# One core of Trainium2, two transformer blocks with a mixture of experts: a narrow expert's transposes moved behind the wide one's second products, seven load buffers filled by halves, norm rows asked for sooner

## Chip, core, metric

The kernel runs on one core of one Trainium2 chip. The metric is the device time of one execution in microseconds; the number that stands for a kernel is the median of its runs. Engines are named as the profile names them: PE (TensorE), DVE (VectorE), ACT (ScalarE), POOL (GpSimd), SP (SyncE). Each takes its instructions in the order in which they stand in its own queue.

## What is computed

256 positions of width 1024 pass through two layers of a first block (a mixer, then a feed-forward part, each closed by a layer norm) and one layer of a second block. Layer 0 has a dense feed-forward part, layer 1 a mixture of 8 experts. All data are fp32. The parts that the change touches, cut down:

```python
def swiglu(x, w1, w3, w2):
    return (silu(x @ w1) * (x @ w3)) @ w2

def moe_swiglu(x, router_w, w1, w3, w2):           # 8 experts, each position uses 2
    top_v, top_i = top_k(x @ router_w, 2)
    combine = sum(one_hot(top_i, 8) * softmax(top_v)[..., None], axis=1)
    return sum(combine[:, e:e + 1] * swiglu(x, w1[e], w3[e], w2[e]) for e in range(8))

for layer in range(2):
    x = layer_norm(ALPHA * x + hybrid_mixer(x, ...), ln1_g[layer], ln1_b[layer])
    f = moe_swiglu(x, ...) if layer else swiglu(x, ...)   # 1024 -> 3584 -> 1024 per expert
    x = layer_norm(ALPHA * x + f, ln2_g[layer], ln2_b[layer])
# second block
x = x + mixer_2(rms_norm(x, norm1_g))
x = x + conv_ffn(rms_norm(x, norm2_g))
return rms_norm(x, final_g)
```

## The kernel before

The program runs straight through: layer 0's mixer (0 to 225 us of the profiled span), its dense feed-forward part (225 to 411), layer 1's mixer (425 to 650), the experts (650 to 1632), the norms behind them (to 1658), the second block's front (to 1782) and its feed-forward part (to the end).

Weights are read from HBM in loads of 2 MB (128 partitions by 4096 numbers) into buffers called `raw`, all issued by SP (`load`, L151). A weight that meets 128 positions or more is split by `split` (L158) into a high part `wH` (cast by ACT, L170) and a low part `wL` (a subtraction, L172, on DVE or on POOL where `hold` says so), and `mm3` (L175) makes three products of them: L176, L177, L178.

The experts go in four groups of two. Of each pair one is wide: it is given 128 slots for positions, uses split weights, and its names are `main`, `hH`, `hL`. The other is narrow: it has 64 slots, takes the raw fp32 weights straight into PE (`side`, L1243, matmuls of L1247), and its names are `nar`, `gx`, `hN`. (One group has an expert with 192 slots instead.) An expert's hidden width of 3584 is cut into seven pieces of 512. A step of `experts` (L1281) does for one piece: two loads and the first products with w1 and w3 (L1302 to L1310); silu on ACT (L1316 wide, L1321 narrow) and the product of the two on DVE (L1317, L1322); then `down`, the second products, of the step before, with a third load `rd` (L1325); then the transposes of this step's result (L1331 wide, L1339 narrow, both recorded at L182), which ACT copies out (`hN`, L1342) or splits. Wide and narrow steps take turns, so a cycle is one of each: six loads. When a narrow step ends its first products, the second products that follow it are those of the wide step ahead of it: 24 matmuls with the name `acc`. A scheduler settles each engine's order from the program and its dependences; `issue_after(x)` binds an instruction behind x if both are on the same engine.

While the experts run there are six buffers, three in the pool `wp` and three in `mp` (L1360).

A layer norm (L258 to L271) runs per half of the positions, `t`: statistics on DVE, the inverse root by `rsqrt` (L184: one DVE operation and POOL's power, L188), then on DVE one operation over 1024 columns (L268) and a pair of 128x512 (L270). `rms` (L286) is alike, with its pair at L300. `layer_norm` and `rms` give back `p`, the rsqrt; `finish` (L312) transposes the result and puts into `hold` that the next splits of weights on POOL come after `p`. This is so at four places: behind the mixer of layer 0, behind its feed-forward part, behind the experts, and in the second block's front. The norm behind the experts takes its rows of gains and offsets by `row` (L273), DMAs that ACT issues: `g` ahead of the branch for overfull experts (L1389), `b` and `g2` behind it (L1396).

## Time and profile before

| | us |
|---|---|
| median of 3 runs | 2001.44 (1994.93 to 2006.64) |
| the profiled execution | 2001.22 |
| its span, first to last instruction | 1999.4 |
| busy: PE, DVE, ACT, POOL | 1819.5, 1197.6, 842.3, 203.4 |
| experts' loads | 168 of 2 MB |

The profile is one execution on the chip. Busy times are sums over an engine's instructions; an engine's idle time counts only where it holds up what sets the end. The rows further down come from six views: the page (shares by engine, DMA issues), waits (how long an engine stood still, and for what), the timeline (instruction by instruction: start, length, engine, line, operation, and in brackets the idle time before it and what ended it), windows (busy time, granted clock of PE and DMA by stretch), groups by line, and the DMA queue's own waits. [...]

### The profile page before, as it was taken

To read this page: it belongs to the slowest core of one execution; us is meant where nothing else is said; L and a number is where in the kernel's file an instruction comes from. 1 tells how busy PE (TensorE), PEld (TensorE's weight loads), DVE (VectorE), ACT (ScalarE), POOL (GpSimd) and SP (SyncE) were. 2 spreads that over 40 slices of the span, in tenths; PEclk is the share of its full clock that TensorE was granted. 3 is DMA by queue.
4 is the path that set the end of the run, shared out by engine and by line. 5 is a ranking of instruction groups with operands and counts; after the bars stand their busy time and mean duration, and the time that the engine had idled before them with its cause. 6 is when DMAs were issued, how large, how long until landed. Compare 5 with 4: busy or idle time off the path is not lost. (4 is left out here: it accounts for less than half of the span.)

```text
span 1999.4 us, 28155 instructions
## 1 busy us (share of the span) xinstructions
PE 1819.5 (91%) x11670; PEld 1408.2 (70%) x11670; DVE 1197.6 (60%) x1717; ACT 842.3 (42%) x1176; POOL 203.4 (10%) x128
## 2 busy tenths in 40 slices
PE   7778899986878999998989999999999868989998
PEld 6666899975656766666666666666666637779997
DVE  6796654578785755355454544344553647667776
ACT  3234344433243545334343443343443525545554
POOL 4251200043323000000000000000000004010000
PEclk9788999998788999999999999999999988799999
DMA  6320536352204799999999777787999944134551
GB/s 241 118 94 23 190 137 243 127 215 85 95 13 169 282 430 418 388 393 355 363 393 384 300 297 305 307 342 315 365 414 390 399 156 164 43 135 171 185 195 64
DMA packets 37574, 484.76 MB, mean 242 GB/s; under 512 B 4544, under 2 KB 5184, under 8 KB 8000
## 3 DMA queue, kind: packets, MB, share of 16 engines
q1 hardware_dynamic: 34992, 475.74, 60.8%
q10 hardware_dynamic: 2448, 7.17, 1.1%
q8 instruction: 93, 1.52, 0.3%
q14 instruction: 41, 0.34, 0.0%
HBM read 481.84 MB, written 1.05 MB: 242 GB/s over the span
## 5 line engine op out<-in xcount | busy, mean ns | idle before, releaser
L172 DVE TENSOR_TENSOR wL<-raw,wH 128x1024 fp32r<-128x1024 f32 (+1 forms) x510 | 616.3, 1229 | 261.9 <-ACT wH L170 250.7
L170 ACT CAST wH<-raw 128x1024 fp32r<-128x1024 f32 x560 | 577.5, 1051 | 401.7 <-PE mm L177 154.0
L1247 PE MATMUL mm<-raw,gx 128*64 128x256 f32 x2240 | 252.3, 381 | 0.0
L1247 PEld LDWEIGHTS mm<-raw,gx 128*64 128x64 f32 x2240 | 156.6, 137 | 85.6 <-issue 10.8
L176 PE MATMUL acc<-wH,hH 128*128 128x512 f32 x408 | 163.8, 416 | 19.8 <-ACT wH L170 19.0
L176 PE MATMUL mm<-wH,g 128*128 128x512 f32 x448 | 177.1, 395 | 0.0
L177 PE MATMUL acc<-wL,hH 128*128 128x512 f32 x408 | 169.7, 416 | 7.2 <-DVE wL L172 7.1
L177 PE MATMUL mm<-wL,g 128*128 128x512 f32 x448 | 175.1, 391 | 0.0
L178 PE MATMUL mm<-wH,g 128*128 128x512 f32 x448 | 174.8, 390 | 0.0
L178 PE MATMUL acc<-wH,hL 128*128 128x512 f32 x408 | 166.8, 410 | 0.0
L172 POOL TENSOR_TENSOR wL<-raw,wH 128x1024 fp32r<-128x1024 f32 x50 | 126.1, 2532 | 135.2 <-ACT wH L170 122.3
L188 POOL TENSOR_TENSOR sm_brs<-sm_brs,half_neg 128x1 f32<-128x1 f32 x8 | 12.1, 1518 | 1207.2 <-DVE sm_brs L186 1207.2
L1247 PE MATMUL acc<-raw,hN 128*64 128x512 f32 x560 | 127.5, 597 | 0.0
L1321 ACT ACTIVATE ff<-mm 128x256 f32<-128x256 f32 x35 | 13.5, 385 | 247.8 <-PE mm L1247 247.8
L176 PEld LDWEIGHTS acc<-wH,hH 128*128 128x128 f32 x408 | 79.1, 197 | 44.4 <-ACT wH L170 22.5
L177 PE MATMUL mm<-b2yL,wH 128*128 128x256 f32 x384 | 109.7, 286 | 0.0
L176 PE MATMUL mm<-b2yH,wH 128*128 128x256 f32 x384 | 109.6, 286 | 0.0
L178 PE MATMUL mm<-b2yH,wL 128*128 128x256 f32 x384 | 109.4, 285 | 0.0
L1322 DVE TENSOR_TENSOR ff<-ff,mm 128x256 f32<-128x256 f32 x35 | 14.7, 421 | 157.2 <-ACT ff L1321 157.2
L177 PEld LDWEIGHTS acc<-wL,hH 128*128 128x128 f32 x408 | 80.2, 197 | 32.3 <-DVE wL L172 14.7
L176 PE MATMUL mm<-y0H,wH 128*128 128x256 f32 x352 | 100.1, 285 | 0.0
L178 PE MATMUL mm<-y0H,wL 128*128 128x256 f32 x352 | 99.8, 284 | 0.0
(518 smaller groups left out, 3263.2 us busy)
## 6 DMA issues: line engine op xcount, KB each, us to landing
raw<-in_moe_dram SPq DMA_DIRECT2D x168, 2048.0 KB, 9.7
raw<-in_ffn_dram SPq DMA_DIRECT2D x33, 2048.0 KB, 7.7
raw<-in_w_in_dram SPq DMA_DIRECT2D x13, 2048.0 KB, 9.2
raw<-in_w_o_dram SPq DMA_DIRECT2D x4, 2048.0 KB, 7.5
row<-in_ln_dram ACTq DMA_DIRECT2D x8, 512.0 KB, 3.6
raw<-in_w_out_dram SPq DMA_DIRECT2D x2, 2048.0 KB, 8.4
raw<-in_w_in_dram SPq DMA_DIRECT2D x3, 1024.0 KB, 5.1
raw<-in_ffn_dram SPq DMA_DIRECT2D x3, 1024.0 KB, 5.2
```

The lines of the kernel that those rows point to most:

```text
L170: self.A.copy(H, src)
L172: (eng or self.V).tensor_tensor(L, src, H.bitcast(F32), OP.subtract)
L176: self.T.matmul(out, lhsT=lh, rhs=rh, start=start, stop=False)
L177: self.T.matmul(out, lhsT=lh, rhs=rl, start=False, stop=False)
L178: return self.T.matmul(out, lhsT=ll, rhs=rh, start=False, stop=stop)
L188: return self.G.tensor_tensor(out, out, self.half_neg.to_broadcast([P, n]), OP.pow)
L1247: T.matmul(out[i * 64:i * 64 + 64], lhsT=lhsT, rhs=rhs[:, i * n:i * n + n], start=start, stop=stop)
L1321: A.activation(sn[-1], b[:, 0:256], AF.Silu)
L1322: V.tensor_tensor(sn[-1], sn[-1], b[:, 256:512], OP.mult)
```

## The change

1. `RAWS` = 4 load buffers in `wp` instead of 3, in the whole kernel. The experts take seven fixed tiles in turn (four of `wp`, three of `mp`), and such a tile is filled by two DMAs of 1 MB.
2. The narrow expert's transposes are bound behind the last matmul of piece j = 2 of the second products that `down` has just put out.
3. Gain and offset of the norm behind the experts go into one tile `gb` by two DMAs ahead of the branch.
4. `p`, behind which POOL's held splits come, is the last DVE operation of the norm instead of the rsqrt on POOL.
5. The program is built with a smaller scratch space for DMAs issued from engines.

```diff
@@ __init__
-        self.raws = [(self.wp, 3)]
+        self.raws = [(self.wp, RAWS)]
@@ load
-        self.nc.sync.dma_start(raw[:, :n], ap)
+        m = n if isinstance(src, tuple) else n // 2
+        for o in range(0, n, m):
+            self.nc.sync.dma_start(raw[:, o:o + m], ap[:, o:o + m])
         return raw
@@ layer_norm
-        p = self.rsqrt(rs, mv[:, 1:2], 1.0, LN_EPS)
+        self.rsqrt(rs, mv[:, 1:2], 1.0, LN_EPS)
         V.scalar_tensor_tensor(r[:, t], r[:, t], mv[:, 0:1], g, op0=OP.subtract, op1=OP.mult)
         for n in range(2):
-            V.scalar_tensor_tensor(r[:, t, half[n]], r[:, t, half[n]], rs, b[:, half[n]], op0=OP.mult, op1=OP.add)
-        return p
+            last = V.scalar_tensor_tensor(r[:, t, half[n]], r[:, t, half[n]], rs, b[:, half[n]], op0=OP.mult, op1=OP.add)
+        return last
@@ rms
         for n in range(2):
-            self.V.scalar_tensor_tensor(dst[:, t, half[n]], xn[:, t, half[n]], ss[:, 0:1], g[:, half[n]], op0=OP.mult, op1=OP.mult)
-            yield half[n]
+            yield self.V.scalar_tensor_tensor(dst[:, t, half[n]], xn[:, t, half[n]], ss[:, 0:1], g[:, half[n]], op0=OP.mult,
+                                              op1=OP.mult)
@@ experts, down
-                            self.mm3(acc[n], h[0][:, j], h[1][:, j], H[:, 0, ns], L[:, 0, ns], *ends)
+                            last = self.mm3(acc[n], h[0][:, j], h[1][:, j], H[:, 0, ns], L[:, 0, ns], *ends)
+                        if j == 2:
+                            state["down"] = last
@@ experts
             for (p, b), s in zip(nar, sn):
-                b = self.bank()
+
+                b, last = self.bank(), state.pop("down", None)
                 for i in range(2):
-                    self.transpose(b[:, i * P:(i + 1) * P], s[:, i * P:(i + 1) * P])
+                    with self.tc.issue_after(last.ins) if last else nullcontext():
+                        self.transpose(b[:, i * P:(i + 1) * P], s[:, i * P:(i + 1) * P])
@@ moe
-        self.raws, self.chunk = [(self.wp, 3)] * 3 + [(self.mp, MORE)] * MORE, 0
+
+        self.raws = [p.tile([P, 4096], F32, tag="raw", name=f"raw{n}x{i}", bufs=n) for p, n in (
+            (self.wp, RAWS), (self.mp, MORE)) for i in range(n)]
+        self.chunk = 0
...
-        self.raws = [(self.wp, 3)]
-        ahead = self.block2_loads(0, 3)
-        g = self.row(a["ln"][1, 2], "rscr")
+        self.raws = [(self.wp, RAWS)]
+        ahead = self.block2_loads(0, RAWS)
+        gb = self.xp.tile([P, 2, D], F32, tag="xTL", name="gb", bufs=1)
+        for i in range(2):
+            A.dma_start(gb[:, i], a["ln"][1, 2 + i].partition_broadcast(P))
...
-        self.raws = [(self.wp, 3)]
-        b, g2 = self.row(a["ln"][1, 3], "yL"), self.row(a["rows2"][0], "yH")
+        self.raws = [(self.wp, RAWS)]
+        g2 = self.row(a["rows2"][0], "yH")
...
-            self.layer_norm(xn, t, g, b)
+            self.layer_norm(xn, t, gb[:, 0], gb[:, 1])
         for t in range(2):
-            p, *_ = self.rms(xn, t, g2, h)
+            *_, p = self.rms(xn, t, g2, h)
@@ block 2, front
-        left = self.block2_loads(3, 4)
+        left = self.block2_loads(RAWS, 4)
...
-            p = next(rms[t])
+            next(rms[t])
         for r in rms:
-            list(r)
+            *_, p = r
```

PE, a cycle of the second group before: `gx` are the narrow expert's first products, `ff` the transposed result, `wH` and `wL` the wide expert's second products.

```order
L1247 MATMUL mm_7794<-raw_7788,gx_7125 64x256 x16
L1247 MATMUL mm_7794<-raw_7790,gx_7125 64x256 x16
L182 MATMUL mm_7870<-cst_4_126,ff_7827 128x128 x2
L176 MATMUL acc_7437<-wH_7830,hH_7784 128x512
L176 MATMUL acc_7438<-wH_7830,hH_7784 128x512
L177 MATMUL acc_7437<-wL_7831,hH_7784 128x512
```

The same cycle after the change (lines are three or seven higher; of the 24 second products the first and the last stand here):

```order
L1250 MATMUL mm_7606<-raw4x_5604,gx_7132 64x256 x16
L1250 MATMUL mm_7606<-raw4x_5605,gx_7132 64x256 x16
L179 MATMUL acc_7444<-wH_7642,hH_7596 128x512
L179 MATMUL acc_7445<-wH_7642,hH_7596 128x512
L180 MATMUL acc_7444<-wL_7643,hH_7596 128x512
...
L181 MATMUL acc_7444<-wH_7672,hL_7597 128x512
L180 MATMUL acc_7445<-wL_7673,hH_7596 128x512
L181 MATMUL acc_7445<-wH_7672,hL_7597 128x512
L185 MATMUL mm_7682<-cst_4_126,ff_7639 128x128 x2
L179 MATMUL mm_7693<-wH_7695,g_7131 128x512
```

The two transposes stand behind all 24 second products instead of ahead of them.

ACT, a cycle of the first group before: L1316 is the wide silu, L1321 the narrow one, L1342 the copy of the transposed narrow result, `wH` from the first raw the casts of the second products' weights.

```order
L1316 ACTIVATE ff_6585<-mm_6503 128x512
L170 CAST hH_6601<-mm_6596 128x512
L1321 ACTIVATE ff_6644<-mm_6611 128x256
L1342 COPY hN_6690<-mm_6687 128x256
L170 CAST wH_6647<-raw_6609 128x1024
L170 CAST wH_6657<-raw_6609 128x1024
L170 CAST wH_6667<-raw_6609 128x1024
L170 CAST wH_6677<-raw_6609 128x1024
L170 CAST wH_6700<-raw_6692 128x1024
```

After:

```order
L1321 ACTIVATE ff_6787<-mm_6705 128x512
L173 CAST wH_6767<-raw3x_5609 128x1024
L173 CAST wH_6777<-raw3x_5609 128x1024
L173 CAST hH_6803<-mm_6798 128x512
L1326 ACTIVATE ff_6846<-mm_6813 128x256
L173 CAST wH_6849<-raw4x_5606 128x1024
L173 CAST wH_6859<-raw4x_5606 128x1024
L173 CAST wH_6869<-raw4x_5606 128x1024
L173 CAST wH_6879<-raw4x_5606 128x1024
L173 CAST wH_6902<-raw3x_5607 128x1024
L173 CAST wH_6912<-raw3x_5607 128x1024
L1349 COPY hN_6892<-mm_6889 128x256
```

The copy moved from ahead of the casts to behind six of them; the casts stay behind the narrow silu.

POOL behind the experts, before: `sm_brs` and `sm_rms` are the rsqrts of the layer norm and of the rms norm, `wL` the two held splits.

```order
L188 TENSOR_TENSOR sm_brs_20595<-sm_brs_20595,half_neg 128x1
L188 TENSOR_TENSOR sm_brs_20606<-sm_brs_20606,half_neg 128x1
L188 TENSOR_TENSOR sm_rms_20612<-sm_rms_20612,half_neg 128x1
L188 TENSOR_TENSOR sm_rms_20618<-sm_rms_20618,half_neg 128x1
L172 TENSOR_TENSOR wL_20681<-raw_12104,wH_20680 128x1024
L172 TENSOR_TENSOR wL_20709<-raw_12104,wH_20708 128x1024
```

After:

```order
L191 TENSOR_TENSOR sm_brs_20603<-sm_brs_20603,half_neg 128x1
L175 TENSOR_TENSOR wL_20687<-raw_12111,wH_20686 128x1024
L175 TENSOR_TENSOR wL_20715<-raw_12111,wH_20714 128x1024
L191 TENSOR_TENSOR sm_brs_20614<-sm_brs_20614,half_neg 128x1
L191 TENSOR_TENSOR sm_rms_20620<-sm_rms_20620,half_neg 128x1
L191 TENSOR_TENSOR sm_rms_20626<-sm_rms_20626,half_neg 128x1
```

Since `p` is now on DVE, nothing binds POOL's two splits any more, and they moved from behind the last rsqrt to behind the first.

## Rows read from the trace of the kernel before

**Rows 1.** The page, busy time of each engine, share of the span, instructions.

```profile
PE 1819.5 (91%) x11670; PEld 1408.2 (70%) x11670; DVE 1197.6 (60%) x1717; ACT 842.3 (42%) x1176; POOL 203.4 (10%) x128
```

**Rows 2.** Waits of PE, 700 to 1625 us: total us, times, longest us.

```profile
PE acc L176 <- ACT wH L170: 19.0, 14, 1.5
PE mm L182 <- DVE ff L1322: 14.1, 15, 0.9
PE acc L177 <- DVE wL L172: 7.1, 14, 0.6
```

**Rows 3.** Timeline, 784.5 to 790: start, us, engine, line, operation, [idle before, releaser].

```profile
785.27 0.38 ACT L1321 ACTIVATE ff<-mm 128x256 f32<-128x256 f32 x1 [6.48 <-PE mm L1247]
785.69 0.42 DVE L1322 TENSOR_TENSOR ff<-ff,mm 128x256 f32<-128x256 f32 x1 [6.17 <-ACT ff L1321]
...
786.16 0.44 PE L182 MATMUL mm<-cst,ff 128*128 128x128 f32 x2 [0.94 <-DVE ff L1322]
...
786.91 3.89 ACT L170 CAST wH<-raw 128x1024 fp32r<-128x1024 f32 x4
...
788.01 0.73 PE L176 MATMUL acc<-wH,hH 128*128 128x512 f32 x2 [1.41 <-ACT wH L170]
...
789.26 0.50 PE L177 MATMUL acc<-wL,hH 128*128 128x512 f32 x1 [0.53 <-DVE wL L172]
```

**Rows 4.** Timeline, 753 to 757.

```profile
753.50 0.38 ACT L1321 ACTIVATE ff<-mm 128x256 f32<-128x256 f32 x1 [6.48 <-PE mm L1247]
753.78 3.88 ACT L170 CAST wH<-raw 128x1024 fp32r<-128x1024 f32 x4
...
754.87 0.73 PE L176 MATMUL acc<-wH,hH 128*128 128x512 f32 x2
```

**Rows 5.** Timeline of ACT, 784 to 850, the next two narrow silus.

```profile
816.85 0.38 ACT L1321 ACTIVATE ff<-mm 128x256 f32<-128x256 f32 x1 [6.48 <-PE mm L1247]
...
849.96 0.38 ACT L1321 ACTIVATE ff<-mm 128x256 f32<-128x256 f32 x1 [6.48 <-PE mm L1247]
```

**Rows 6.** Windows: length, busy PE PEld DVE ACT POOL, PEclk, DMA share, GB/s.

```profile
740.00:760.00 20.00, 18.49 (x108) 11.04 (x107) 6.95 (x8) 6.06 (x8) 0.00 (x0) 0.91 1.01 431
...
960.00:980.00 20.00, 17.61 (x99) 11.39 (x96) 8.01 (x8) 7.70 (x10) 0.00 (x0) 0.83 0.95 378
...
1200.00:1300.00 100.00, 100.00 (x617) 64.03 (x617) 39.79 (x39) 34.94 (x44) 0.00 (x0) 1.00 0.78 305
...
1500.00:1520.00 20.00, 17.66 (x112) 10.52 (x110) 4.58 (x6) 4.47 (x7) 0.00 (x0) 1.00 0.99 396
```

**Rows 7.** Groups by line, 700 to 1625: the casts | busy, mean ns | idle before, releasers.

```profile
L170 ACT CAST wH<-raw 128x1024 fp32r<-128x1024 f32 x311 | 319.0, 1052 | 86.4 <-PE acc L178 48.2 <-PE mm L178 35.9 <-DMA raw<-in_moe_dram 2.0
```

**Rows 8.** Waits of SP's DMA queue, 700 to 1650 us.

```profile
SPq L155 <- DVE wL L172: 338.5, 56, 24.6
SPq L155 <- PE mm L1247: 308.7, 66, 9.6
```

**Rows 9.** The page, DMA issues: KB each, median us from issue to landing.

```profile
raw<-in_moe_dram SPq DMA_DIRECT2D x168, 2048.0 KB, 9.7
...
raw<-in_ffn_dram SPq DMA_DIRECT2D x3, 1024.0 KB, 5.2
```

**Rows 10.** Timeline of DVE, 211 to 225, behind layer 0's mixer.

```profile
213.16 1.41 DVE L270 SCALAR_TENSOR_TENSOR xn<-xn,sm_brs,row 128x512 f32<-128x512 f32 x2
...
218.63 5.50 DVE L270 SCALAR_TENSOR_TENSOR xn<-xn,sm_brs,row 128x512 f32<-128x512 f32 x2
```

**Rows 11.** Timeline of POOL, 211 to 225.

```profile
217.00 1.52 POOL L188 TENSOR_TENSOR sm_brs<-sm_brs,half_neg 128x1 f32<-128x1 f32 x1 [3.94 <-DVE sm_brs L186]
218.50 5.09 POOL L172 TENSOR_TENSOR wL<-raw,wH 128x1024 fp32r<-128x1024 f32 x2
```

**Rows 12.** Timeline of DVE, 1639 to 1657, behind the experts.

```profile
1643.38 1.41 DVE L270 SCALAR_TENSOR_TENSOR xn<-xn,sm_brs,row 128x512 f32<-128x512 f32 x2 [2.47 <-DMA row<-in_ln_dram]
...
1650.75 5.58 DVE L300 SCALAR_TENSOR_TENSOR h<-xn,sm_rms,row 128x512 f32<-128x512 f32 x2 [0.66 <-POOL sm_rms L188]
```

## The prediction, made before the changed kernel ran

> **What bounds the kernel now.** I read four views, in this order. The page's first part shows TensorE (PE) busy for 91% of the span, VectorE (DVE) for 60%, ScalarE (ACT) for 42% and GpSimd (POOL) for 10% [rows 1]. So time is to be had only where PE stands still or runs slow. The view of PE's waits over the experts (700 to 1625 us) comes second: PE stood 40.2 us there, 19.0 for the high part of a split weight (`wH`, cast on ACT), 14.1 for the narrow expert's product `ff` ahead of its transposes (L182), 7.1 for the low part `wL` [rows 2]. No load is among the names: the casts on ACT lost 2.0 us to `raw` in all [rows 7], and SyncE's queue waits for buffers to come free (338.5 us for DVE, 308.7 for PE) [rows 8]. Third, the timeline of one such place tells how the 40.2 us arise. The narrow first products end; ACT's silu L1321 starts at 785.27, DVE's L1322 follows, then PE's two transposes at 786.16 (0.94 idle). ACT, in its own order, makes the copy `hN` next and only at 786.91 the first cast of the weights for the wide expert's second products; PE gets them at 788.01 (1.41 idle) and the first `wL` at 789.26 (0.53 idle) [rows 3]. That is 2.88 us; fourteen such places, one of them short, and 1614 make up the view's sum. Last, the rows by 20 us: the granted clock is 1.00 where PE works without a gap, and 0.91 or 0.83 in nine bins (eight like the first row, one like the second) [rows 6], each behind one or several gaps.

> **The change part by part.**

> *Transposes behind the second products.* Today's chain from the end of the narrow products is silu, DVE, transposes, copy, cast. After the change PE's row has the 24 second products between the narrow products and the transposes, and ACT's row has silu, then casts, then the copy. A place of before shows that very order on ACT: at 753.50 the silu, at 753.78 the cast, and PE had its `wH` at 754.87 [rows 4], 1.37 us behind the silu's start. At 785.27 that gives 786.64 instead of 788.01: 1.37 us sooner, less the 0.44 of transposes, which PE now does later, so 0.93 us a place. The 0.53 for `wL` stays, and 1.4 us behind the silu stays. The order on ACT is of this kind in thirteen cycles: the third of the first group, six of the second, four of the third pair with a narrow expert of 64 slots: 13 × 0.93 = 12. At the first place (753) the casts stand ahead of the silu altogether, so its 0.94 + 0.53 go: 1.5. In the last place two DMA issues for the norm rows stand on ACT; I take half a microsecond back for them. Sum −12.1 − 1.5 + 0.5, **−13**. Moved work is covered: the transposes' result is needed only after the next 48 first products. The bounds: −17 if the 0.53 goes too in half the places, −5 if the copy or the casts' data come late.

> *Clock.* A cycle without a fall takes 816.85 − 785.27 = 31.58 us, one with a fall 849.96 − 816.85 = 33.11 [rows 3, 5]: 1.5 us a fall. Nine bins, one of them double, are ten falls [rows 6], 15 us. With gaps of 1.4 + 0.5 instead of 0.9 + 1.4 + 0.5 some falls should go. I take a third, **−5**, with 0 and −15 as the ends, because before shows gaps of 2.88 with and without a fall in the next bins and none as short as those to come.

> *Seven buffers, filled by halves.* Sequence: a load waits for a buffer, not PE for a load [rows 7, 8]. A cycle moves six loads of 2 MB, 12.58 MB. After the change it lasts 31.58 − 0.93 = 30.7 us and needs 410 GB/s; the best bins moved 431 [rows 6], which is a floor of 29.2 us. So more buffers have nothing to win here, and I take **0**. Halves add some 168 issues on SyncE's queue, which waits anyway. A whole load of 2 MB took 9.7 us from issue to landing and one of 1 MB 5.2 [rows 9], so a half costs about half. [...]

> *Norm ends.* Two GpSimd splits (5.1 us together) stood behind the last rsqrt at four places; DVE's pair of 128x512 operations took 1.41 us alone and 5.5 beside them (213.16 and 218.63 at the first place, 1650.75 at the third; the other two read alike) [rows 10 to 12]. With the hold now tied to DVE's last operation, GpSimd is free to take the splits between the first rsqrt and the second; the order shows it. The slow pair then becomes the first, and the second rsqrt waits for the splits' end. Place 1 (212): first pair +4.1, second −4.1: 0. Place 2 (412 to 424): the last pair gives back 4.1; the first, slower by 4.1, has PE's last second products still running beside it, and I take some half of its loss as covered: −2.3. Place 3 (1640 to 1656): today 2.47 of waiting for a norm row and 5.58 in the last pair; the row is on hand since it is asked for before the branch : the first pair starts about 2.2 sooner and takes 4.1 longer, so what follows comes 1.9 later; the last pair gives back 4.2: −2.3. Place 4 (1769 to 1781): last pair −4.1, the second rsqrt, which finds the splits ahead of it, pushed by half of their 5.1: −1.6. Sum **−6**. Bounds: −9 (all slow pairs covered) and +4 (nothing gained, and each second rsqrt late by 1.1: the two pairs start 5.47 apart, and splits of 5.09 and an rsqrt of 1.52 now have to fit between [rows 10, 11]). What the statistics on DVE cost beside a GpSimd split no row shows; by the nearest, the pair at 1.41 against 5.5, it is between nothing and 2.3 us a place; I take nothing, and the +4 has room for it. [...]

> *Four load buffers elsewhere.* The front of layer 1's mixer (425 to 650) is written the same but comes out in another order on PE and DVE. I find no row that prices it: **0**, with 4 us to either side (about 2% of that stretch).

> Sum: −13 − 5 + 0 − 6 + 0 = −24. The profiled execution took 2001.22 us (its span 1999.4 and some 2 around it, which no part touches), the median of the runs is 2001.44, 0.2 more; so **1977 us**, 1.2% less.

> **The rivals.**

> *All falls go.* If the shorter gaps leave the clock at its higher level throughout, another 10 us go: 1967. For it: 1200 to 1300, where PE has no gap, shows no fall [rows 6]. Against it: the gaps at 753, with 1.5 us in sum, have a fall in their bin [rows 4, 6].

> *Casts stay the limit.* The gap becomes one gap of 1.4 + 0.5 rather than three, and the falls stay, or new ones come; the norm ends give nothing because the splits now delay the second rsqrt. Then −13 + 6 or so is left: some 1994, within 0.5%.

> *The halves cost, and the end is slower.* The cycle needs 12 halves in 30.7 us, one each 2.56 us. If a half costs more than that in the steady flow, the experts become bound by loads; the point from which it decides is 2.56 us. At 431 GB/s a half is 2.43 us, so it must lose over 0.13 to get there. At 2.9 us (0.47 lost in each half) a cycle takes 34.8 us, 3.2 more than today's 31.58; over some fourteen such cycles +45: 2046. Rows for it: no stretch with 1 MB loads back to back exists in the trace, and the DMA engines' share is 0.99 already at 396 GB/s [rows 6], so little is idle. Against it: 1 MB loads landed in 5.2 us [rows 9], and a seventh buffer leaves one more load in flight.

> *It doesn't do what it says.* The order on PE and ACT shows that it does.

> **How the numbers follow.** Forecast 1977: 0.57. All falls go, 1967: 0.14. Casts or splits eat the gain, about 1994: 0.19. Loads bind, 2046: 0.05. The last 0.05 goes to the mixer of layer 1 or another place costing more than it is given here. A measurement of this kernel tells about 0.5% (10 us) from no change. Faster by over 0.5% (below 1991): the first two and a third of the third, 0.78; within: 0.15; slower: 0.07. The range from 1960 to 1997 holds the first three; it leaves out the loads' case and the fifth.

> **What would show it.** Right: PE no longer waits for `ff` ahead of the transposes; PE waits for `wH` some thirteen times at about 1.4 us; silus of the narrow expert 30.7 us apart; fewer bins below 1.00; no wait for a norm row at 1640; the last pair of DVE at each norm end back at 1.41 us and the first at about 5.5. Wrong: PE or ACT waiting for `raw` in the experts (the loads), `hN` late for the narrow second products, or the stretch from 425 to 650 longer by over 4 us.

## The result, and the profile after

| | us |
|---|---|
| before, median of 4 runs | 2001.9 (1994.9 to 2006.6) |
| after, median of 4 runs | 1970.07 (1965.3 to 1976.9) |
| after : before | 0.985, 95% interval 0.982 to 0.987 |
| forecast | 1977 (1960 to 1997) |

The change is worth 32 us (1.5%); the median is 7 below the forecast. The profiled execution of after is the longest of the four (1976.9; span 1975.1 against 1999.4 of before), so only 24.3 of the 32 are in the two traces. Its mean granted clock was 0.944, that of the other three 0.947 to 0.951. Where these 24.3 went, from the first matmul of each part to the first of the next: from the start to the second gather of the first group of experts +1.4 (686.2 to 687.7), the experts from there to the last scatter products 941.1 to 919.7, **−21.4**; from there to the second block's first product −3.3; the rest −1.0. Lines of the changed kernel are three to seven higher than those of before.

PE's waits in the experts, 690 to 1610 (total us, times, longest), answering [rows 2]:

```profile
PE acc L179 <- ACT wH L173: 20.0, 14, 1.6
PE acc L180 <- DVE wL L175: 8.2, 16, 0.6
PE mm L1176 <- ACT gx L1186: 0.8, 1, 0.8
```

The wait for `ff` ahead of the transposes (14.1) is gone, the two others are as they were: 29 us in all instead of 41. One place, answering [rows 3] (start, length, [idle before, releaser]):

```profile
784.66 0.39 ACT L1326 ACTIVATE ff<-mm 128x256 f32<-128x256 f32 x1 [6.48 <-PE mm L1250]
784.94 4.83 ACT L173 CAST wH<-raw3x 128x1024 fp32r<-128x1024 f32 x5
785.07 0.42 DVE L1327 TENSOR_TENSOR ff<-ff,mm 128x256 f32<-128x256 f32 x1 [6.17 <-ACT ff L1326]
...
786.03 0.73 PE L179 MATMUL acc<-wH,hH 128*128 128x512 f32 x2 [1.42 <-ACT wH L173]
...
787.29 0.51 PE L180 MATMUL acc<-wL,hH 128*128 128x512 f32 x1 [0.53 <-DVE wL L175]
```

From the silu's start to PE's first `wH` it is 1.37 us, where it was 2.74; the cast stands right behind the silu. The granted clock, answering [rows 6] (length, busy PE PEld DVE ACT POOL, PEclk, which is that clock as a share of full speed, DMA share, GB/s): of the 20-us bins from 700 to 1600 two are at 0.95 or less, where nine were. A bin of the first group, then the two:

```profile
740.00:760.00 20.00, 20.00 (x124) 12.90 (x123) 9.26 (x10) 7.68 (x10) 0.00 (x0) 1.00 1.01 421
```

```profile
980.00:1000.00 20.00, 18.06 (x107) 11.12 (x104) 8.57 (x9) 6.74 (x8) 0.00 (x0) 0.91 1.00 398
1460.00:1480.00 20.00, 18.05 (x108) 11.58 (x105) 8.11 (x8) 6.95 (x9) 0.00 (x0) 0.91 1.01 421
```

The norm ends, answering [rows 10 to 12]. Behind the experts, on DVE, the slow pair is the first one now, and its wait for the row is gone:

```profile
1619.71 5.56 DVE L273 SCALAR_TENSOR_TENSOR xn<-xn,sm_brs,gb 128x512 f32<-128x512 f32 x2 [0.31 <-POOL sm_brs L191]
...
1631.23 1.42 DVE L303 SCALAR_TENSOR_TENSOR h<-xn,sm_rms,row 128x512 f32<-128x512 f32 x2 [0.66 <-POOL sm_rms L191]
```

Behind layer 0's feed-forward part it is another story. POOL's splits had to wait there for ACT's casts, so they began only when the first pair was nearly done:

```profile
415.81 4.90 POOL L175 TENSOR_TENSOR wL<-raw,wH 128x1024 fp32r<-128x1024 f32 x2 [1.23 <-ACT wH L173]
420.68 1.52 POOL L191 TENSOR_TENSOR sm_brs<-sm_brs,half_neg 128x1 f32<-128x1 f32 x1
```

```profile
414.70 1.41 DVE L273 SCALAR_TENSOR_TENSOR xn<-xn,sm_brs,row 128x512 f32<-128x512 f32 x2
416.02 0.69 DVE L266 BATCH_NORM_STATS2 sm_bst<-xn 128x6 f32<-128x512 f32 x1
...
418.51 3.29 DVE L271 SCALAR_TENSOR_TENSOR xn<-xn,sm_bmv,row 128x1024 f32<-128x1024 f32 x1
```

The same operations in the trace of before, without a split beside them:

```profile
415.43 0.69 DVE L263 BATCH_NORM_STATS2 sm_bst<-xn 128x6 f32<-128x512 f32 x1
...
416.48 1.28 DVE L268 SCALAR_TENSOR_TENSOR xn<-xn,sm_bmv,row 128x1024 f32<-128x1024 f32 x1
```

The pair took 1.41, the statistics 0.69 with the splits and without, and only the operation over 1024 columns, on `xn` and a row, went from 1.28 to 3.29.

### The profile page after: what moved, and what is told of

It is laid out like the page before. It is cut to its first block, busy times and chain, and to the rows that moved or that the text cites. A ratio compares the mean times of both kernels' runs of the same rounds, so it can differ in the third digit from the quotient of the medians.

```text
span 1975.1 us, 28866 instructions
## 1 busy us (share of the span) xinstructions
PE 1815.8 (92%) x11670; PEld 1401.1 (71%) x11670; DVE 1198.0 (61%) x1717; ACT 835.3 (42%) x1176; POOL 201.6 (10%) x128
## 3 DMA queue, kind: packets, MB, share of 16 engines
q8 instruction: 93, 1.52, 0.3%
## 5 line engine op out<-in xcount | busy, mean ns | idle before, releaser
L173 ACT CAST wH<-raw 128x1024 fp32r<-128x1024 f32 (+1 forms) x224 | 232.5, 1049 | 292.2 <-PE mm L180 160.7
L175 DVE TENSOR_TENSOR wL<-raw,wH 128x1024 fp32r<-128x1024 f32 (+1 forms) x174 | 213.2, 1233 | 154.7 <-ACT wH L173 154.5
L175 DVE TENSOR_TENSOR wL<-raw4x,wH 128x1024 fp32r<-128x1024 f32 x192 | 227.5, 1222 | 63.6 <-ACT wH L173 56.8
L173 ACT CAST wH<-raw4x 128x1024 fp32r<-128x1024 f32 x192 | 194.0, 1050 | 40.7 <-PE acc L181 24.2
L175 DVE TENSOR_TENSOR wL<-raw3x,wH 128x1024 fp32r<-128x1024 f32 x144 | 171.2, 1222 | 47.0 <-ACT wH L173 44.9
L179 PE MATMUL acc<-wH,hH 128*128 128x512 f32 x408 | 156.2, 407 | 20.7 <-ACT wH L173 20.0
L173 ACT CAST wH<-raw3x 128x1024 fp32r<-128x1024 f32 x144 | 145.7, 1050 | 25.3 <-PE acc L181 13.0
L1250 PE MATMUL mm<-raw4x,gx 128*64 128x256 f32 x1280 | 145.3, 381 | 0.0
L191 POOL TENSOR_TENSOR sm_brs<-sm_brs,half_neg 128x1 f32<-128x1 f32 x8 | 12.1, 1517 | 1179.7 <-PE mm L312 974.9
L1250 PEld LDWEIGHTS mm<-raw4x,gx 128*64 128x64 f32 x1280 | 89.3, 137 | 49.1 <-issue 7.1
L1250 PE MATMUL mm<-raw3x,gx 128*64 128x256 f32 x960 | 108.9, 382 | 0.0
```

Of the source, the lines that this page charges most:

```text
L173: self.A.copy(H, src)
L175: (eng or self.V).tensor_tensor(L, src, H.bitcast(F32), OP.subtract)
L179: self.T.matmul(out, lhsT=lh, rhs=rh, start=start, stop=False)
L191: return self.G.tensor_tensor(out, out, self.half_neg.to_broadcast([P, n]), OP.pow)
L1250: T.matmul(out[i * 64:i * 64 + 64], lhsT=lhsT, rhs=rhs[:, i * n:i * n + n], start=start, stop=stop)
```

## The experiments

"Idle" is PE's waiting for `ff`, `wH` and `wL` in the experts, "falls" the number of 20-us bins from 700 to 1600 with a granted clock of 0.95 or less inside the experts, "experts" the time from the second gather of their first group to the last scatter products. Ratios are against the kernel before on the same chip.

| kernel | us | ratio | idle | falls | experts |
|---|---|---|---|---|---|
| before | 2001.9 | | 40.2 | 9 | 941 |
| after | 1970.1 | 0.982 to 0.987 | 28.2 | 2 | 920 |
| x1 transposes alone | 1976.5 | 0.983 to 0.990 | 30.1 | 2 | 917 |
| x2 all but the transposes | 2005.3 | 0.999 to 1.003 | 39.8 | 8 | 946 |
| x3 whole loads | 1971.1 | 0.980 to 0.987 | 28.3 | 2 | 917 |
| x4 held splits | 1974.1 | 0.983 to 0.989 | 28.2 | 2 | 918 |
| x5 gaps filled | 1988.1 | 0.993 to 0.998 | 23.1 | 0 | 933 |
| x8 rows alone | 2003.0 | 1.000 to 1.005 | 39.3 | 12 | 947 |
| x6 one cast first | 1951.1 | 0.976 to 0.981 | 9.9 | 0 | 897 |
| x7 same, whole loads | 1954.7 | 0.974 to 0.981 | 13.7 | 0 | 898 |
| x11 same as x6, six buffers | 1949.5 | 0.976 to 0.979 | 9.9 | 1 | 898 |
| x9 two casts first | 1937.9 | 0.966 to 0.972 | 2.7 | 1 | 887 |
| x10 same, whole loads | 1932.0 | 0.962 to 0.968 | 3.5 | 1 | 884 |
| x12 two casts, on the kernel before | 1935.6 | 0.966 to 0.971 | 0.9 | 0 | 880 |

### One part alone, one part undone

**x1**: the kernel before with the `state["down"]` lines and the bound transposes of the diff, nothing else.

> The kernel before with the moved transposes alone (six buffers, whole loads, norm rows and held splits as before). Theory: the gaps behind the narrow products shrink from 40 us to some 28 us of PE idle between 700 and 1625, and since a gap is shorter the clock falls in three or fewer 20-us bins there instead of nine; time 2001 - 12 - 12 = about 1977. Rival, the loads: the falls go because of seven buffers and halves, not because of the gaps; then 28 us of idle, but seven or more falls, and about 1989.

1976.5: the theory's number. PE's waits, 690 to 1630:

```profile
PE acc L176 <- ACT wH L170: 21.6, 16, 1.4
PE acc L177 <- DVE wL L172: 8.5, 16, 0.6
```

and two bins with a fall. So the moved transposes give 25 of the 32 us by themselves, and the falls go with them, whatever the buffers and loads are.

**x2**: the changed kernel with these lines taken out.

```diff
-                b, last = self.bank(), state.pop("down", None)
+                b = self.bank()
                 for i in range(2):
-                    with self.tc.issue_after(last.ins) if last else nullcontext():
-                        self.transpose(...)
+                    self.transpose(...)
```

> The changed kernel with the narrow transposes where they were. Theory: some 40 us of idle in the experts, nine or ten falls; only the norm ends are gained (6 to 7 us): about 1994. Rival, the loads: the falls stay away, about 1982.

The idle time and the falls came back as the theory has it:

```profile
PE acc L179 <- ACT wH L173: 18.4, 13, 1.5
PE mm L185 <- DVE ff L1325: 13.2, 14, 0.9
PE acc L180 <- DVE wL L175: 8.2, 14, 1.4
```

That settles the rival: seven buffers and halves don't keep the clock up. But 2005 is 11 more than I expected; without the transposes the rest is worth nothing, or costs some 4. The norm ends are as fast in x2's trace as in after's (stretches below), so part of the loss lies in the experts, 946 against 941. There a block of 48 first products took 11.1 us before and 11.3 here (means of 19 blocks outside the third group, 3 us in all). In most of these blocks the difference stands at one place, three quarters through, where two matmuls start 0.33 us behind the one ahead of them instead of 0.23.

The trace by itself would suggest a faster kernel, for the traced execution is the shortest of x2's twelve (1991.6). It had a higher clock: 0.944 in the mean, the other eleven 0.933 to 0.940. It shows in the second block's front, where x2 (first line) and after (second) run the same program:

```profile
1660.00:1762.00 102.00, 91.27 (x551) 78.99 (x550) 77.27 (x130) 63.70 (x123) 19.67 (x17) 0.96 0.37 136
```

```profile
1634.00:1746.00 112.00, 100.54 (x547) 85.07 (x547) 76.20 (x128) 62.82 (x122) 19.63 (x17) 0.87 0.34 123
```

With the 112 us of after in place of its 102, the traced execution would have taken some 2002, like the others (1999 to 2009). The rest of the distance to 1994 can't be told from the spread that the clock makes outside the experts: one and the same program ahead of the first gather took between 645.7 and 655.4 us in the traces of before, x1, x5, x8 and x12.

**x3**: whole loads in the seven buffers (`m = n` in `load`).

> The changed kernel with seven buffers, but each filled by one load of 2 MB. Theory: the loads are not what PE waits for, so 1970 within 4 us, with 28 us of idle and two or three falls. Rival: halves let a buffer be refilled sooner and that is part of the gain: over 1976, and PE or ACT waiting for raw in the experts. Other side: the steady rate of halves was 421 GB/s against 431 of whole loads; if that binds in the first group, it becomes faster, about 1965.

1971, as the theory: no difference that the medians can tell. The rate differs, as the first of the two lines (x3) and the second (after) show for the first group, and PE's busy share there doesn't:

```profile
700.00:800.00 100.00, 98.05 (x539) 69.10 (x534) 57.25 (x54) 50.99 (x59) 0.00 (x0) 1.00 1.01 428
```

```profile
700.00:800.00 100.00, 98.05 (x538) 69.14 (x535) 56.13 (x52) 50.19 (x59) 0.00 (x0) 1.00 1.01 419
```

In the traces the halves still cost something. PE's waits and the falls are the same in both, but two narrow silus are 30.5 us apart in x3 (first fence) and 30.8 in after (second), and the experts take 917 us instead of 920:

```profile
784.51 0.39 ACT L1327 ACTIVATE ff<-mm 128x256 f32<-128x256 f32 x1 [6.48 <-PE mm L1251]
...
814.98 0.39 ACT L1327 ACTIVATE ff<-mm 128x256 f32<-128x256 f32 x1 [6.48 <-PE mm L1251]
```

```profile
784.66 0.39 ACT L1326 ACTIVATE ff<-mm 128x256 f32<-128x256 f32 x1 [6.48 <-PE mm L1250]
...
815.46 0.38 ACT L1326 ACTIVATE ff<-mm 128x256 f32<-128x256 f32 x1 [6.48 <-PE mm L1250]
```

The blocks of 48 first products account for it: 11.2 us in x3, 11.3 to 11.4 in after. x9 and x10 below differ by the same 3 us.

**x4**: `p` is the rsqrt again, so POOL's splits are held.

```diff
-        self.rsqrt(rs, mv[:, 1:2], 1.0, LN_EPS)
+        p = self.rsqrt(rs, mv[:, 1:2], 1.0, LN_EPS)
...
-            *_, p = self.rms(xn, t, g2, h)
+            p, *_ = self.rms(xn, t, g2, h)
```

> The changed kernel with p the rsqrt on POOL again, so that POOL's two splits are held behind the last rsqrt at the four norm ends. Theory: place 2 loses 2.2 us, place 4 1.8 us, place 1 gains 0.4, place 3 stays (its gain of 3.3 us comes from the norm rows asked for sooner): 3.5 us slower, about 1974. Rival: place 3's gain comes from the splits' new place as well: 6 to 7 us slower, about 1977.

1974, where 1974 was expected; 4 us are within what the runs leave open, but the stretches at the norm ends repeat to a tenth in the traces. From the norm's statistics (places 1 and 2), from the last scatter product (3), and from the first rms rsqrt (4) to the next part's first product, in us:

| place | before | x8 (rows alone) | x4 (rows, held) | after (rows, free) |
|---|---|---|---|---|
| 1, behind layer 0's mixer | 14.69 | 14.69 | 14.70 | 15.13 |
| 2, behind its feed-forward part | 14.81 | 14.81 | 14.81 | 12.64 |
| 3, behind the experts | 25.35 | 21.71 | 21.74 | 22.05 |
| 4, second block's front | 13.53 | 13.52 | 13.53 | 11.71 |

Moving the splits costs 0.4 at the first place and 0.3 at the third, and gives 2.2 at the second and 1.8 at the fourth: 3.3. The rows give 3.6 at the third.

**x8**: the kernel before with `gb` alone.

> The kernel before with gain and offset of the norm behind the experts asked for ahead of the branch, and nothing else. Theory: the wait of 2.47 us for the row goes, and the stretch from the branch to the norm's statistics, 4.5 us before and 3.0 after the change, shrinks by 1.5: 3 to 4 us faster, about 1996 against 1999 to 2001, which is at the edge of what can be told; the trace tells by the stretch from the last scatter product to the second block's first product (29.9 us before, 26.5 after). Rival: the row isn't what the end waits for, the stretch stays at 29 us.

The stretch shrank by 3.6 us, as the theory has it, and the pair no longer waits for a row:

```profile
1642.31 1.42 DVE L270 SCALAR_TENSOR_TENSOR xn<-xn,sm_brs,gb 128x512 f32<-128x512 f32 x2 [0.31 <-POOL sm_brs L188]
```

Yet the time was 2003, not 1996. The experts, whose program is the same as before's, took 947 us in its trace instead of 941: twelve bins with a fall instead of nine, and two of them double.

```profile
1060.00:1080.00 20.00, 17.62 (x85) 12.66 (x82) 11.19 (x11) 10.85 (x12) 0.00 (x0) 0.83 0.98 391
1540.00:1560.00 20.00, 17.62 (x98) 11.41 (x95) 8.11 (x8) 7.93 (x10) 0.00 (x0) 0.83 0.98 390
```

At 1.5 us a fall the four more (a double bin counts as two) eat the gain. The same program of the experts had ten falls in the trace of before and fourteen in this one; I can't say why one cycle has one and the next has none.

### The falls priced by themselves

**x5**: the kernel before with five matmuls on zeros behind the narrow transposes, in the second of the three gaps.

```diff
-            hs = {}
+            pend_hs, hs = (hs if pend else {}), {}
...
+                if 0 in pend_hs and p == 1 and not main:
+                    self.warm(5, self.tlast)
                 h = self.mp.tile([P, 2, P], F32, tag="hN", name=f"hN{self.n}", bufs=1)
```

> The kernel before with five matmuls on zeros (1.1 us, result unused) behind the narrow transposes, where PE waited 1.4 us for wH; nothing else is moved, so the wait itself is as long as before. It prices the clock falls apart from the gaps. Theory: the falls come with PE standing still, so filled gaps leave the granted clock at 1.00; nine bins with falls become two or three and the time drops by 1.5 us for each of the eight falls gone: about 1989. Rival: the falls have another cause (the mix of work, the transfers) and stay: 2001, or up to 5 us more for the extra matmuls.

The place at 785, PE alone: the chain is as long as in [rows 3] (second products at 788.05, there 788.01), only 1.4 us of it are filled.

```profile
786.20 0.44 PE L183 MATMUL mm<-cst,ff 128*128 128x128 f32 x2 [0.94 <-DVE ff L1323]
786.40 1.39 PE L310 MATMUL mm<-zero 128*128 128x512 f32 x5
788.05 0.74 PE L177 MATMUL acc<-wH,hH 128*128 128x512 f32 x2 [0.26 <-ACT wH L171]
```

And no fall is left:

```profile
700.00:900.00 200.00, 194.86 (x1094) 132.37 (x1094) 100.85 (x117) 82.66 (x104) 0.00 (x0) 1.00 1.00 411
900.00:1100.00 200.00, 188.83 (x1044) 130.05 (x1041) 101.79 (x106) 90.57 (x114) 0.00 (x0) 1.00 0.97 388
1400.00:1600.00 200.00, 194.53 (x1061) 131.61 (x1061) 100.37 (x97) 83.75 (x97) 0.00 (x0) 1.00 0.97 392
```

1988.1 against 1998.6 of before on that chip: 10.5 us for work that is thrown away. So the falls come from PE standing still (nine bins of before, none with the second gap filled). The 10.5 us are net of what the fill costs where PE did not wait there: in four such cycles narrow silus are 28.4 or 29.3 us apart instead of 27.3 or 28.2, 4.5 us in all. The falls alone are then worth some 15 us, the ten of before at 1.5.

### What is left: the casts behind the silu

After still waits 1.42 + 0.53 in each place, since ACT makes the narrow silu ahead of the casts. **x6** makes the first split of the second products' weights ahead of it and binds the silu behind that cast; **x7** adds whole loads, **x11** six buffers instead of seven; **x9** makes two splits first, **x10** with whole loads. The diff is that of x9 (`self.cast` is the last cast that `split` has made).

```diff
+            pre = None
+            if nar and not main and pend and 0 in hs:
+                r4 = rd.rearrange("p (f d) -> p f d", d=D)
+                pre = [self.split(r4[:, q:q + 1], (1, D)) for q in range(2)]
...
             for p, b in nar:
...
-                A.activation(sn[-1], b[:, 0:256], AF.Silu)
+                with self.tc.issue_after(self.cast.ins) if pre else nullcontext():
+                    A.activation(sn[-1], b[:, 0:256], AF.Silu)
...
-                        H, L = self.split(rd[:, j:j + 1], (1, D))
+                        H, L = pre[j] if pre and j < 2 else self.split(rd[:, j:j + 1], (1, D))
```

> The changed kernel, and the first cast of the second products' weights stands ahead of the narrow silu on ACT in every cycle, so that PE finds wH when its narrow products end. Theory: the gap of 1.4 + 0.5 goes in 13 cycles, but the loads become the bound: at 421 GB/s (the flat rate of halves in the first group) a cycle of 12.58 MB lasts 29.9 us instead of 30.75, so 11 us are won, about 1959, and PE or ACT wait for raw. Rival: the loads don't bind, the cycle becomes 28.8, 25 us are won, about 1945. Other rival: the cast waits for its load and the silu behind it comes late, no gain, 1970.

> The same with whole loads of 2 MB in the seven buffers. Theory: where loads bind, whole loads at 428 to 431 GB/s give a cycle of 29.2 to 29.4 us, 0.5 to 0.7 less than with halves, over some 13 cycles 6 to 9 us: about 1951. Rival: halves free parts of a buffer sooner and that outweighs the rate, as fast as x6 or slower by up to 5 us.

x6: 1951, between the two. One place of it: PE's `wH` is there when the narrow products end (no idle time in the first line), the silu comes behind.

```profile
943.97 0.73 PE L179 MATMUL acc<-wH,hH 128*128 128x512 f32 x2
...
944.09 0.39 ACT L1331 ACTIVATE ff<-mm 128x256 f32<-128x256 f32 x1 [5.54 <-PE mm L1250]
...
946.72 0.51 PE L180 MATMUL acc<-wL,hH 128*128 128x512 f32 x1 [0.53 <-DVE wL L175]
```

The 1.42 went, the 0.53 only moved on to the second unit; cycle 29.3 us. That the loads would bind was wrong: ACT waited 1.9 us in sum for `raw`. x7 is the same within its interval.

> As the kernel with the casts first, but two casts and their subtractions stand ahead of the narrow silu, which takes the last half microsecond of waiting (for wL) out of each cycle. On PE alone a cycle would be 28.8 us; six loads at the 421 GB/s of halves need 29.9. Theory: the loads now bind, PE or ACT wait for raw for several us in the first two groups, and only some 3 of the 7 us are won: about 1948. Rival: the store of seven full buffers covers the lack, all 7 are won: about 1944. Other rival: the casts wait for their loads ahead of the silu and hold the narrow transposes up: 1951 or more.

> The same with whole loads: 428 GB/s, 29.4 us a cycle. Theory: less waiting for raw than with halves, 2 to 4 us faster than those, about 1945. Rival: as halves or slower, since a whole buffer has to be free before its load begins.

Both did better than any of my cases. PE's waits of x10, 690 to 1570, and its first stretches:

```profile
PE acc L180 <- ACT wH L174: 2.1, 1, 2.1
PE acc L181 <- DVE wL L176: 1.4, 2, 0.9
```

```profile
700.00:800.00 100.00, 100.00 (x569) 68.58 (x569) 54.50 (x52) 46.03 (x54) 0.00 (x0) 1.00 1.01 427
800.00:900.00 100.00, 100.00 (x564) 67.55 (x560) 54.53 (x74) 42.62 (x58) 0.00 (x0) 1.00 1.01 428
900.00:1000.00 100.00, 100.00 (x578) 69.90 (x577) 57.22 (x55) 50.27 (x60) 0.00 (x0) 1.00 1.01 427
```

A cycle takes 28.2 us there, and 12.58 MB in 28.2 us are 446 GB/s, more than the 427 to 428 that these stretches moved. The buffers make up for it: at 428 GB/s a cycle is short of 0.5 MB, six cycles of 3 MB. Counted from x10's trace (loads landed less loads used by PE and DVE), five loads of 2 MB are on hand at 900 us, early in the second group, and 3.4 at 1040, behind the last of its cycles of 28.2 us. That floor of mine was a floor for an endless row of cycles, not for six.

> The kernel with one cast first, with six buffers (four and two) filled by halves instead of seven. Theory: since loads run nearly without a pause there (421 GB/s for 400 us), a buffer less costs about the time of one load at each group that starts full, up to 5 us in all: about 1955, and ACT or PE wait for raw. Rival: six are enough, 1951.

1949.5: six are enough. Waits for a load show on DVE, and nothing that is late on PE follows from them (PE's waits are those of x6):

```profile
DVE wL L175 <- DMA raw2x<-in_moe_dram: 16.9, 5, 4.1
```

> The kernel before (six buffers, whole loads, old norm ends) with the moved transposes and two casts ahead of the narrow silu: what the shortest version is worth. Against the fastest so far (1932, seven buffers with whole loads) it lacks the norm ends, 6.9 us by the stretches of the traces, and a seventh buffer. Theory: six buffers cost up to 5 us where loads run without a pause, seen as waits for raw on ACT or DVE of over 5 us in the first two groups: 1939 to 1944. Rival: the seventh buffer is worth nothing: 1939 and no such waits. Other rival: with a cycle of 28.2 us and 12.58 MB, six buffers make the experts bound by loads at 431 GB/s, 29.2 us a cycle: 1950.

1935.6, better than all cases. The same count gives 3.5 loads on hand at 900 us and 1.5 at 1040, so less is left here. From 700 to 1000 us, with six buffers and whole loads, the loads ran without a pause and PE stood still nowhere:

```profile
700.00:1000.00 300.00, 300.00 (x1707) 206.06 (x1706) 166.22 (x179) 137.83 (x171) 0.00 (x0) 1.00 1.01 430
```

So neither the seventh buffer nor the halves earn anything. x10 has the lower median (1932.0 against 1935.6), their intervals overlap, and the faster norm ends, 6.9 us by the stretches above, should be most of its lead. Against that x12 gains 4.5 us in the last group, where x10 has a wait of 2.1 and a fall in its last place.

## Why the prediction was right, and where it was off

- **Transposes, −13 forecast.** Right in place and size. PE's idle time fell by 12 us, each place lost the 0.94 and kept 1.42 + 0.53 [rows 3], cycles without a fall last 30.7 to 30.8 us (784.66 to the next narrow silu at 815.46), and at the first three narrow steps of the first group PE has no gap. (The thirteen cycles of the sum are three of the first group, at 785, 817 and 850 us, six and four; "the third" of the first group would make eleven.) That the cycle came out as forecast (30.7) has some luck in it: the transposes took it to 30.4 to 30.5 (x1, x3), and the halves gave 0.3 back.
- **Clock, −5 forecast.** The term that was mis-sized. Ten falls became two: 8 × 1.5 = 12 us, as the first rival had it; x5 prices the same falls at 10.5 net of its fill. I gave a third because before showed no gap as short as those to come, yet the place at 753, which I held against the rival, has gaps of 1.5 us, shorter than the 1.95 of after. One fall there showed that such gaps can bring a fall, not how often: in after two places in fourteen did. Take the rival's size here, and the sum gives 2001 − 13 − 12 − 6 = 1970, the median that was measured. That it fits to the microsecond is luck: the halves cost 3, the norm ends gave 1 more, and the traced executions differ by 24.3 only.
- **Seven buffers and halves, 0 forecast.** Right for the buffers (x11, x12), and for the halves as far as the medians can tell (x3); in the traces halves cost some 3 us of the experts, on PE and not by a wait for `raw`. Halves ran at 421 GB/s and whole loads at 427 to 431, so halving cost 2% of the rate where loads are queued one behind the other.
- **Norm ends, −6 forecast.** 6.9 measured (−6.9 = +0.4 − 2.2 − 3.3 − 1.8; forecast 0, −2.3, −2.3, −1.6). At the third place the sign of a part was off: the splits' new place costs 0.3, and the whole gain is the rows asked for sooner, which also took 1.5 us out of the way from the branch to the statistics. At the second place the first pair was not slow at all, since ACT's casts came late.
- **Statistics on DVE beside POOL, taken at nothing.** Right: 0.69 beside the splits at the second place, as without them. No row of before showed it; to take nothing out of the range of 0 to 2.3 us was the author's estimate. The operation over 1024 columns did lose there, 3.29 us against 1.28.
- **Layer 1's mixer, 0 ± 4.** From its first product to the experts' first gather 223.5 us before and 223.9 after.
- **The slower rival, loads.** Its deciding point, 2.56 us a half, was never reached (2.49 at 421 GB/s), and it was no point: x10 went below its floor for six cycles at a time.

What stays open: why the clock outside the experts differs from one execution to the next, by 10 us of one and the same program; why one gap brings a fall and the next, alike, doesn't; and why a block of 48 first products takes 0.2 us longer with halves.

## To carry to other kernels

When an engine that sets the end stands still in short gaps, price the gap and the clock's fall behind it apart: here the second was as large as the first (12 us each), and filling the gap with useless work alone won 10 us where removing part of it won 25. A step off the path (the narrow transposes) that stood ahead of the next long stretch in its engine's order cost its whole chain of releases here (0.94 us of waiting in each place, 25 us with the falls, x1); move such a step behind that stretch, and do the same on the engine that feeds it (the casts ahead of the silu), which here gave as much again or more (32 us with halves, x9; 38 with whole loads, x10). Deep buffers turned a rate limit into a limit on a long average here (x10: six cycles that used 446 GB/s from loads at 427 to 428), so test a load floor over the number of cycles that there are.

## What the runs showed of the hardware

```profile
757.00:759.00 2.00, 2.00 (x7) 1.52 (x6) 2.00 (x3) 1.97 (x3) 0.00 (x0) 0.50 0.95 410
```

- Loads from HBM ran at 430 GB/s for 300 us while PE was busy without a pause (x12, 700 to 1000), and queued 1 MB loads at 421 (after, 740 to 760).
- A DVE pair of 128x512 operations on a row and `xn` took 5.49 to 5.58 us beside two POOL subtractions at the four places of before, and 1.41 to 1.42 without (213 and 1769 us). In after it took 5.58 and 5.56 beside them at the first and the third place, 3.56 at the fourth. At the second place of after an operation over 1024 columns took 3.29 beside them, against 1.28 in before, and the statistics 0.69 with or without.
